# A decoder layer's index scores for the sample: TensorE in written order, with projections in pieces of three matmuls between transposes, products and head sums

## The chip, the core and the metric

The kernel runs on one core of a Trainium2 chip. The core has five engines with a queue each: PE (TensorE, matrix products and transposes), DVE (VectorE), ACT (ScalarE), POOL (GpSimd) and SP (which only issues transfers here). The metric is the device time of one execution in microseconds (us), the median of several runs.

## The reference, cut to what matters

One step of a hybrid decoder layer: 1024 tokens of a prompt and 8 samples of 4 new tokens with 8192 old keys each. The stage in question computes, for the sample's tokens, the index scores by which the 256 best keys are chosen; the same is done for the prompt.

```python
def _index_select(qi, wi, ki, qpos, kpos, topk):
    s = jnp.einsum('bqhd,bsd->bqhs', qi, ki) * (D_IDX ** -0.5)
    score = jnp.einsum('bqh,bqhs->bqs', wi, jax.nn.relu(s))
    valid = kpos[None, None, :] <= qpos[None, :, None]
    score = jnp.where(valid, score, -jnp.inf)
    top_val, top_idx = lax.top_k(score, topk)
    return top_idx, jnp.isfinite(top_val)

def _dsa_sample(qa, ka, va, qi, ki, wi, cache_k, cache_v, cache_kidx, page_table, rel_bias):
    ki_past = cache_kidx[page_table].reshape(B, past, D_IDX)
    ki_all = jnp.concatenate([ki_past, ki], axis=1)
    idx, ok = _index_select(qi, wi, ki_all, qpos, kpos, topk)
    ...
```

Ahead of it stand the RMSNorm and one input projection (`z = h @ w_in`, split into `qa, ka, va, qi, ki, wi, ga, qb, kb, vb, gb`); behind it the attention over the chosen keys, the retention heads, gates, output projection and a gated embedding.

## The kernel before, in words

A scheduler (Tile) puts the written instructions into an order for each engine, by priorities and its own estimates; where the program says `issue_after`, it pins one behind another. Every engine then works through its list without looking ahead: an instruction that waits holds up all behind it.

The stage is the loop over 8 samples `b` and two halves `a` (L797 to L838), 16 half-iterations. A half-iteration gathers 128 pages of index keys with a GpSimd transfer (`kx`, L801), turns them on PE in two blocks of 8 transposes (`ptx`, L810; a PSUM pair, two of them), copies each block to SBUF on ACT (`kT`, L811; two buffers), and multiplies with the queries in 8 matmuls (`pox`, L817). These fill two PSUM banks, the even matmuls one and the odd ones the other; ACT applies relu to each bank (`rl`, L826). After two half-iterations the heads are summed: `head_sum`, 4 matmuls into `py` (L772, L775), an ACT copy `ys`, a store to `xt_d`; and later `by_key`: 4 transposes `pxt` (L784), 8 small copies `xe` on DVE (L789), a store to `xs_d`. The two are kept in a list `pend` and one is taken out per half-iteration (`later`).

PSUM has two banks of the kind "t" at this time. `pox` takes both, and `pxt`, and the transposes `kvt` of the key and value projections (L404, inside `use_kv`), take one each. So a `pxt` bank has to be emptied by DVE's `xe` before the `pox` that comes next can write into it.

Beside this two other chains run. The unit generator (`units`) projects `qa`, `ka` and `va`, and `ga`, each a `triple` of three groups of tokens (384, 384 and 288 wide), each group 24 matmuls `pb` (`proj_b`, L252 to L254: high times high, high times low, low times high). `unit(1.4)` takes 1.4 groups out of it per half-iteration. The generator `bp` (`bisect_prompt`) finds the prompt's thresholds bit by bit: 15 bits, each with 4 counts on DVE (L663), two sign counts `js` on ACT (L659), a fix-up (L667), and the next candidate (L682, L684); then a tail, nearly all on DVE: low words and maxima (L696, L698, L704), a branch (L713), and for each of six blocks of 384 to 1024 keys the final mask (L731 to L738, with the scan L735 and L736 behind it). `step(bp)` takes one step, two per half-iteration.

After the loop the sample's own search begins (`bisect_sample`), which loads `xt_d`, and the retention projections follow on PE (`pqk`, L271 and L262 to L264).

Of the kernel before, what the change touches and what calls it, by code (L numbers as in the profile page):

```python
# [22 lines left out]
NS = 32  # L23
# [97 lines left out]
def tile_step(ctx: ExitStack, tc: tile.TileContext, I, O):  # L121
# [5 lines left out]
    psum = {}  # L127

# [63 lines left out]
    def make_toep(tz):  # L192
# [8 lines left out]
        nc.tensor.matmul(pt[:, :384], rb16.rearrange("p r h -> p (r h)"), onehot, start=True, stop=True)  # L201
# [41 lines left out]
    def proj_b(w, c0, m, consume, groups=(0, 1, 2)):  # L243

        hi, lo = w[:2]
        for g in groups:
# [3 lines left out]
            for k in range(KC):  # L250
                wh, wl = hi[:, k, c0:c0 + m], lo[:, k, c0:c0 + m]
                nc.tensor.matmul(pt[:m, :n], wh, xh[:, k, ts], start=(k == 0), stop=False)  # L252
                nc.tensor.matmul(pt[:m, :n], wh, xl[:, k, ts], start=False, stop=False)
                nc.tensor.matmul(pt[:m, :n], wl, xh[:, k, ts], start=False, stop=(k == KC - 1))  # L254
            consume(g, pt)

    def mm_a(pt, lhs, w, n, tb, kc=KC):

        hi, lo = w[:2]
        for k in range(kc):  # L260
            ah, al = lhs(k, tb)
            nc.tensor.matmul(pt[:, :n], ah, hi[:, k, :n], start=(k == 0), stop=False)  # L262
            nc.tensor.matmul(pt[:, :n], ah, lo[:, k, :n], start=False, stop=False)  # L263
            nc.tensor.matmul(pt[:, :n], al, hi[:, k, :n], start=False, stop=(k == kc - 1))  # L264

    def mm_s(pt, a, w, n, sp, name, kc=KC):

        ng = min(4, kc)
        for k in range(kc):
            j = k % ng  # L270
            nc.tensor.matmul(pt[NS * j:NS * j + NS, :n], a[:, k, :], w[2][k], start=(k < ng), stop=(k >= kc - ng))  # L271
# [75 lines left out]
    def mm_qk(pt, st, kh, kl, n):  # L347
        for c in range(0, n, 512):
            w = min(512, n - c)
            nc.tensor.matmul(pt[:, c:c + w], st, kh[:, c:c + w], start=True, stop=False)  # L350
            nc.tensor.matmul(pt[:, c:c + w], st, kl[:, c:c + w], start=False, stop=True)
# [44 lines left out]
    def use_kv(g, pt, outs, outp, new):  # L396
# [3 lines left out]
        nc.scalar.copy(st[:, 0, :n], pt[:, :n])  # L400
        tp = bank("kvt", "t")
        for i in range(0, n, 128):
            rows = min(128, n - i)
            nc.tensor.transpose(tp[:rows, i:i + 128], st[:, 0, i:i + rows], ident)  # L404
# [7 lines left out]
        return tk  # L412
# [12 lines left out]
    def use_va(g, pt):  # L425
        tk = use_kv(g, pt, O["v_sample"], O["v_prompt"], vnew)
        nc.sync.dma_start(v_d[:, 3 * g:min(8, 3 * g + 3), :], tk)
# [34 lines left out]
    with pool("ix", side="right") as ix:  # L462
# [4 lines left out]
        def use_ki(g, pt):  # L467
# [6 lines left out]
            for i in range(0, n, 128):  # L474
                tb, rows = g * 3 + i // 128, min(128, n - i)
                tp = bank("kt", "t")
                nc.tensor.transpose(tp[:rows, :72], kiT[:, i:i + rows], ident[:72, :72])
# [281 lines left out]
    for h in range(8):  # L759
        nc.tensor.matmul(pn[:NS, h * 32:h * 32 + 32], qsn[:, h, :], kis, start=True, stop=True)  # L760
# [8 lines left out]
    def head_sum(b, rls):  # L769
        py = bank("py")  # L770

        last_ = nc.tensor.matmul(py[96:128, :], wst[:, b, :], rls[3], start=True, stop=True)  # L772
# [8 lines left out]
    def by_key(b, ys):  # L781
        pt = bank("pxt", "t")
        for i in range(4):
            nc.tensor.transpose(pt[:, i * 128:(i + 1) * 128], ys[:, i * 128:(i + 1) * 128], ident)  # L784
# [8 lines left out]
    def later():  # L793
        if pend:
            pend.pop(0)()

    for b in range(8):  # L797
        rls = []
        for a in range(2):
# [4 lines left out]
            kTs = []  # L804
            for up in range(2):
                pt = pair("ptx")
                kT = sx.tile([128, 1024], F32, tag="kT", bufs=2, name="kT")
                for i in range(8):
                    r2 = up * 8 + i
                    nc.tensor.transpose(pt[:, i * 128:i * 128 + 128], kx[:, r2 * 128:(r2 + 1) * 128], ident)  # L810
                nc.scalar.copy(kT, pt)  # L811
                kTs.append(kT)
            po = [bank("pox", "t") for _ in range(2)]

            def part(e, r):
                rr = slice(64 * r, 64 * r + 64)
                return nc.tensor.matmul(po[r][32 * e:32 * e + 32, :], qbd[rr, b, :],  # L817
                                        kTs[e // 2][rr, e % 2 * 512:e % 2 * 512 + 512], start=True, stop=True)

            first = part(3, 1)  # L820
            with tc.issue_after(first.ins):
                for e, r in ((3, 0), (2, 1), (2, 0), (1, 1), (1, 0), (0, 1), (0, 0)):
                    part(e, r)
            for r in range(2):
                rl = sx.tile([128, 512], F32, tag="rl", bufs=6, name="rl")
                nc.scalar.activation(rl, po[r], AF.Relu)  # L826
                rls.append(rl)
            later()
# [4 lines left out]
            unit(1.4)  # L833
        pend.append(lambda b=b, rls=rls: head_sum(b, rls))
    while pend:
        later()
    for _ in unit_gen:
        step(bp)  # L838
# [5 lines left out]
    def bisect_sample():  # L844
# [26 lines left out]
        def count(thr, op):  # L871
# [3 lines left out]
            nc.tensor.matmul(t, group, cnt, start=True, stop=True)  # L875
# [7 lines left out]
        def totals():  # L883

            t = bank("stot", "t")[:, 0:4]
            nc.tensor.matmul(t, groupr, sgn, start=True, stop=True)
# [77 lines left out]
        nc.tensor.matmul(t[:, :32], group, apart.rearrange("p a b -> p (a b)"), start=True, stop=True)  # L964
# [38 lines left out]
        nc.tensor.matmul(tot, group, cnt, start=True, stop=True)  # L1003
# [3 lines left out]
        for src, dst in ((tf, tq), (need, nq)):  # L1007
            t = bank("tbc", "t")
            nc.tensor.transpose(t[:, :NS], src.to_broadcast([NS, 128]), ident[:NS, :NS])
# [54 lines left out]
    def chunk_mm(qk, vv, tb, rows, mask_ap, hp):  # L1064

        r = bank("ret", "c")
        nc.tensor.transpose(r[:, 0:rows], qk[:rows, 0:128], ident[:rows, :rows])
        nc.tensor.transpose(r[:, 128:128 + rows], qk[:rows, 128:256], ident[:rows, :rows])
# [6 lines left out]
        for j, sc in enumerate((r[:rows, 256:256 + rows], e[:rows, :rows])):  # L1075
            js = slice(j * 64, j * 64 + 64)
            nc.tensor.matmul(sc, qkT[js, 128:128 + rows], qkT[js, 0:rows], start=True, stop=True)
# [40 lines left out]
    def ret_sample(hp, qk, sh, acc):  # L1118
# [7 lines left out]
        for b in range(8):  # L1126
            o = r[NS * (b % 4):NS * (b % 4) + NS, 0:128]
            nc.tensor.matmul(o, qm[:, b, :], s0[:, b, :], start=(b < 4), stop=(b >= 4 and b % 4 > 1))
        for j in range(2):
            nc.tensor.matmul(r[NS * j:NS * j + NS, j * 64:j * 64 + 64], sm[:NS, j, :NS], vv[:NS, j * 64:j * 64 + 64],  # L1130
# [5 lines left out]
        for j in range(2):  # L1136
# [4 lines left out]
            nc.tensor.matmul(d[js], qk[:NS, 128 + j * 64:192 + j * 64], vm, start=True, stop=True)  # L1141
# [28 lines left out]
    def sample_select():  # L1170
# [41 lines left out]
        def prefix(src):  # L1212
# [8 lines left out]
            nc.tensor.matmul(t[:, :NS], low, tot, start=True, stop=True)  # L1221
# [23 lines left out]
        for c in range(0, NS * 66, 512):  # L1245
            w = min(512, NS * 66 - c)
            t = bank("pdf", "t")
            nc.tensor.matmul(t[:, :w], dif16, flat[0][:, c:c + w], start=True, stop=True)
# [3 lines left out]
        for q3 in range(0, NS, 3):  # L1252
            nqs = min(3, NS - q3)
            t = bank("psl", "t")
            for i in range(nqs):
# [3 lines left out]
                for a in range(2):  # L1259
                    nc.tensor.matmul(t[:, (2 * i + a) * 66:(2 * i + a + 1) * 66],  # L1260
# [16 lines left out]
        for g in range(2):  # L1277
# [4 lines left out]
            nc.tensor.matmul(t[:, :1], t8.rearrange("p q h -> p (q h)"), C("far"), start=True, stop=True)  # L1282
# [18 lines left out]
    def sample_attn():  # L1301
# [16 lines left out]
        def attend(p):  # L1318
# [21 lines left out]
            for j in range(2):  # L1340
                nc.tensor.transpose(t[:, j * 128:j * 128 + 128], kw[:, j, :128], ident)
# [474 lines left out]
```

## Time and profile before

| what | us |
|---|---|
| median of 3 runs | 1086.92 (1085.57 to 1087.62) |
| the profiled execution, its own time | 1089.05 |
| its span | 1087.3 |
| PE busy in it | 996.1 (92%) |
| DVE busy | 705.1 (65%) |
| ACT busy | 501.5 (46%) |

The profiled execution is one run, so its rows are to be set against its own span; it took 2.1 us more than the median. Its mean granted TensorE clock is 0.95. In rows of the timeline the first number is the start in us from the span's beginning, the second the duration; at the end, in brackets, the idle time before and what ended it. The stage lies between about 182 and 353 us.

### The profile page before, as it was taken

How to read it: one execution, taken by the hardware profiler on the slowest of the kernel's cores; microseconds unless marked ns; L12 is line 12 of the kernel's file. 1: busy time of each engine (PE TensorE's matmuls, PEld its weight loads, DVE VectorE, ACT ScalarE, POOL GpSimd, SP SyncE). 2: the span in 40 equal slices, each digit the busy share in tenths (PEclk: the TensorE clock that was granted, in tenths of full speed). 3: DMA queues.
4: the chain of work that ended last, by engine and by line, in shares of the span. 5: the costliest groups of instructions: out<-in, count | busy, mean ns of one | idle time of the engine just before them, and what ended most of it. 6: DMA issues, size and time to landing. Idle time of an engine off the chain costs nothing.

```text
span 1087.3 us, 19979 instructions
## 1 busy us (share of the span) xinstructions
PE 996.1 (92%) x7499; PEld 846.3 (78%) x7499; DVE 705.1 (65%) x2062; ACT 501.5 (46%) x1090; POOL 288.8 (27%) x285
## 2 busy tenths in 40 slices
PE   3899997888988899988999996899999899999998
PEld 2899997656865898888897884566665799999998
DVE  6847778888890566967969847677763422684332
ACT  5545564866434377532342336556554332452210
POOL 3102223102211432434613512525332321122110
PEclk8899999888988999989999995999999899999999
DMA  8211235435442411112301624524212511332211
GB/s 283 66 59 49 78 107 184 146 128 178 157 143 98 100 40 40 50 32 85 80 4 46 166 95 117 143 73 122 59 44 61 143 59 40 116 119 84 83 42 40
DMA packets 98310, 102.26 MB, mean 94 GB/s; under 512 B 21346, under 2 KB 88386, under 8 KB 95906
## 3 DMA queue, kind: packets, MB, share of 16 engines
q1 hardware_dynamic: 92450, 74.74, 23.0%
q0 software_dynamic: 5760, 26.22, 7.8%
q8 instruction: 59, 0.97, 0.4%
q14 instruction: 41, 0.34, 0.1%
HBM read 79.25 MB, written 21.68 MB: 93 GB/s over the span
## 4 chain that ended last, share of the span: by engine, by line
PE 46%; DVE 11%; issue 5%; DMA 4%; POOL 3%; ACT 3%; SPq 1%; DVEq 0%; POOLq 0%; ACTq 0%
PE pg L262 3%; PE pg L264 3%; PE pg L263 3%; PE pvg L262 3%; PE po L264 3%; PE po L262 3%; PE po L263 3%; PE ob L1592 3%; PE pvg L263 2%; PE pvg L264 2%; PE ptp L1584 2%; DMA wraw_vgb<-in_w_in 1%; PE sa L1568 1%; PE pty L1639 1%; POOL kvs L1159 1%
## 5 line engine op out<-in xcount | busy, mean ns | idle before, releaser
L1159 POOL DMA_INDIRECT kvs<-in_cache_kv,idx x64 | 64.9, 1014 | 86.2 <-ACT pT L1589 32.6
L262 PE MATMUL po<-whi_o,yTh 128*128 128x256 f32 x256 | 74.8, 292 | 4.2 <-DVE x L1679 3.7
L262 PE MATMUL pvg<-whi_vgb,xh 128*128 128x256 f32 x256 | 76.6, 299 | 2.1 <-ACT sg L1061 1.3
L262 PE MATMUL pqk<-whi_qkb,xh 128*128 128x256 f32 x256 | 75.2, 294 | 2.6 <-DVE rp L1048 2.4
L264 PE MATMUL pvg<-whi_vgb,xl 128*128 128x256 f32 x256 | 74.9, 292 | 0.0
L263 PE MATMUL pvg<-wlo_vgb,xh 128*128 128x256 f32 x256 | 74.3, 290 | 0.0
L264 PE MATMUL po<-whi_o,yTl 128*128 128x256 f32 x256 | 74.2, 291 | 0.0
L263 PE MATMUL po<-wlo_o,yTh 128*128 128x256 f32 x256 | 73.9, 289 | 0.0
L264 PE MATMUL pqk<-whi_qkb,xl 128*128 128x256 f32 x256 | 73.8, 288 | 0.0
L263 PE MATMUL pqk<-wlo_qkb,xh 128*128 128x256 f32 x256 | 73.0, 285 | 0.0
L262 PE MATMUL pg<-whi_g,yTh 128*128 128x256 f32 x256 | 72.7, 284 | 0.0
L264 PE MATMUL pg<-whi_g,yTl 128*128 128x256 f32 x256 | 72.3, 282 | 0.0
L263 PE MATMUL pg<-wlo_g,yTh 128*128 128x256 f32 x256 | 72.3, 282 | 0.0
L496 DVE SCALAR_TENSOR_TENSOR score<-r,wi,score 128x384 f32<-128x384 f32 (+5 forms) x42 | 44.2, 1053 | 20.7 <-ACT r L492 19.6
L1577 ACT ACTIVATE L<-L,mn 128x128 f32<-128x128 f32 (+7 forms) x64 | 49.5, 776 | 14.3 <-DVE mn L1574 14.1
L262 PEld LDWEIGHTS po<-whi_o,yTh 128*128 128x128 f32 x256 | 50.4, 197 | 6.0 <-DVE x L1679 3.9
L262 PEld LDWEIGHTS pqk<-whi_qkb,xh 128*128 128x128 f32 x256 | 49.4, 193 | 6.9 <-issue 5.5
L1773 DVE TENSOR_TENSOR sgm<-pu,sgm 128x256 f32<-128x256 f32 x32 | 13.6, 424 | 62.3 <-PE pu L264 55.1
L262 PEld LDWEIGHTS pvg<-whi_vgb,xh 128*128 128x128 f32 x256 | 49.3, 192 | 5.1 <-ACT sg L1061 1.8
L264 PEld LDWEIGHTS pqk<-whi_qkb,xl 128*128 128x128 f32 x256 | 49.1, 192 | 2.7 <-issue 2.4
L1584 PEld LDWEIGHTS ptp<-cst,L 128*128 128x128 f32 x288 | 31.9, 142 | 24.3 <-issue 19.6
L263 PEld LDWEIGHTS po<-wlo_o,yTh 128*128 128x128 f32 x256 | 50.2, 196 | 0.5 <-issue 0.4
(546 smaller groups left out, 3277.5 us busy)
## 6 DMA issues: line engine op xcount, KB each, us to landing
wraw_qkb<-in_w_in SPq DMA_DIRECT2D x16, 256.0 KB, 4.3
wraw_vgb<-in_w_in SPq DMA_DIRECT2D x16, 256.0 KB, 4.2
wraw_o<-in_w_out SPq DMA_DIRECT2D x8, 512.0 KB, 5.5
qas<-qas_d SPq DMA_DIRECT2D x8, 512.0 KB, 5.0
xr<-in_x_prompt SPq DMA_DIRECT2D x8, 512.0 KB, 3.8
wraw_g<-in_w_ple_gate SPq DMA_DIRECT2D x8, 512.0 KB, 4.3
out_y_prompt<-sgm SPq DMA_DIRECT2D x32, 128.0 KB, 1.7
qas_d<-qst SPq DMA_DIRECT2D x8, 384.0 KB, 2.4
```

The source lines that it names most:

```text
L262: nc.tensor.matmul(pt[:, :n], ah, hi[:, k, :n], start=(k == 0), stop=False)
L263: nc.tensor.matmul(pt[:, :n], ah, lo[:, k, :n], start=False, stop=False)
L264: nc.tensor.matmul(pt[:, :n], al, hi[:, k, :n], start=False, stop=(k == kc - 1))
L496: nc.vector.scalar_tensor_tensor(sc, r[:, :n], wi[:, qb, h:h + 1], sc, op0=ALU.mult, op1=ALU.add)
L1159: return nc.gpsimd.indirect_dma_start(out=dst, out_offset=None, in_=kvflat, in_offset=bass.IndirectOffsetOnAxis(ap=idx, axis=0))
L1568: nc.tensor.matmul(s[:, :wc], qas[:, h, :], kah[kv][:, c:c + wc], start=True, stop=False)
L1577: behind[0] = nc.scalar.activation(L[:, :n], L[:, :n], AF.Exp, bias=least, scale=-1.0, accum_out=sm[:, i4:i4 + 1])
L1584: nc.tensor.transpose(tp[:, i4 * 128:i4 * 128 + 128], P[i4][:, kb * 128:kb * 128 + 128], ident)
L1592: nc.tensor.matmul(ob[64 * o:64 * o + 64, :256], vtok[:, kb, kv * 64:kv * 64 + 64], pT[:, o * 256:o * 256 + 256], start=(kb == 0), stop=(k ...
L1639: nc.tensor.transpose(pt[:, j * 128:(j + 1) * 128], src[a][:, j * 128:(j + 1) * 128], ident)
L1773: nc.vector.tensor_tensor(sg[:rows], usrc, sg[:rows], op=ALU.mult)
```

## The change: order and size of the pieces

1. `matmul` and `transpose` are wrappers now. While `pinned[0]` is set, which it is from before the loop to after its tail, each TensorE instruction keeps the order in which it is written. (In the order of the changed kernel all of them bear the lines of the wrappers, L131 and L135.)
2. `triple` yields after every three matmuls, that is 8 times a group; `unit(rate)` outside the stage counts eight pieces for one, so nothing changes there.
3. `use_kv` copies the projection and leaves its transposes, `turn_kv`, in a list `held`; a later piece (the one with k = 2) takes one out.
4. The loop's body is written in the order in which PE is to work, with `fill(n)` laying n pieces in between, 8.4 in a half-iteration. The tail takes the rest of the pieces and the last head sums in turn.
5. The parts of `pox` and `py` stand in plain order, where one of them had been pinned ahead of the rest.

The number of TensorE instructions is the same. The diff, cut (the many lines that only turn `nc.tensor.matmul` into `matmul` are left out):

```diff
+    def matmul(*a, **k):
+        i = nc.tensor.matmul(*a, **k)
+        return tc.keep_in_program_order(i) if pinned[0] else i
...
-        tp = bank("kvt", "t")
+        held.append(lambda: turn_kv(g, st, outs, outp, new))
+
+    def turn_kv(g, st, outs, outp, new):
...
         def triple(w, c0, use):
             for g in range(3):
-                proj_b(w, c0, 128, use, (g,))
-                yield
+                pt = bank("pb")
+                t0, n = GRP[g]
+                ts = slice(t0, t0 + n)
+                for k in range(KC):
+                    wh, wl = w[0][:, k, c0:c0 + 128], w[1][:, k, c0:c0 + 128]
+                    matmul(pt[:, :n], wh, xh[:, k, ts], start=(k == 0), stop=False)
+                    matmul(pt[:, :n], wh, xl[:, k, ts], start=False, stop=False)
+                    matmul(pt[:, :n], wl, xh[:, k, ts], start=False, stop=(k == KC - 1))
+                    if k == KC - 1:
+                        use(g, pt)
+                    elif k == 2 and held:
+                        held.pop(0)()
+                    yield
...
     def unit(rate):
-        tick[0] += rate
+        tick[0] += 8 * rate
...
-        last_ = nc.tensor.matmul(py[96:128, :], wst[:, b, :], rls[3], start=True, stop=True)
-        with tc.issue_after(last_.ins):
-            for i in range(3):
-                nc.tensor.matmul(py[32 * i:32 * i + 32, :], wst[:, b, :], rls[i], start=True, stop=True)
+        for i in range(4):
+            matmul(py[32 * i:32 * i + 32, :], wst[:, b, :], rls[i], start=True, stop=True)
...
+    pinned[0] = True
+    fill(8)
     for b in range(8):
         rls = []
         for a in range(2):
...
+            kTs = [turn(kx, 0)]
+            fill(3)
+            kTs.append(turn(kx, 1))
+            fill(2)
+            if pend:
+                pend.pop(0)()
+            fill(1.7)
+            score_keys(b, kTs, rls)
+            fill(1.7)
             tickb[0] += 2
             while tickb[0] >= 1:
                 tickb[0] -= 1
                 step(bp)
-            unit(1.4)
         pend.append(lambda b=b, rls=rls: head_sum(b, rls))
-    while pend:
-        later()
-    for _ in unit_gen:
-        step(bp)
+    for n, _ in enumerate(unit_gen):
+        if n % 4 == 3 and pend:
+            pend.pop(0)()
+    step(bp, 8)
+    while held:
+        held.pop(0)()
+    while pend:
+        pend.pop(0)()
+    pinned[0] = False
```

`turn` holds the 8 transposes and the `kT` copy, `score_keys` the 8 products and two relus that stood in the loop.

Two places show what the scheduler makes of it. The first is PE, from the fourth `pxt` to the products that follow. Before (`ptx` are the page transposes, `py` the head sum, `pb` the projections, `pox` the products):

```order
L810 MATMUL ptx<-cst,kx 128x128 x4
L784 MATMUL pxt<-cst,ys 128x128 x4
L810 MATMUL ptx<-cst,kx 128x128 x12
L772 MATMUL py<-rl,wst 32x512
L775 MATMUL py<-rl,wst 32x512 x3
L252 MATMUL pb<-xh,whi_ga_2428 128x384
L253 MATMUL pb<-xl,whi_ga_2428 128x384
L254 MATMUL pb<-xh,wlo_ga_2429 128x384
...
L817 MATMUL pox<-kT,qbd 32x512 x8
```

Twenty projections, twelve transposes and a head sum stand between `pxt` and `pox`. In the changed kernel, at its fourth `pxt`:

```order
L131 MATMUL pb<-xl,whi_ga_1742 128x384
L131 MATMUL pb<-xh,wlo_ga_1743 128x384
L135 MATMUL pxt<-cst,ys 128x128 x4
L131 MATMUL pb<-xh,whi_ga_1742 128x384
...
L131 MATMUL pox<-kT,qbd 32x512 x8
L131 MATMUL pb<-xh,whi_ga_1742 128x384
...
L135 MATMUL ptx<-cst,kx 128x128 x8
```

Six projections stand between the two there, and the transposes and the head sum have moved away from the place.

The second is DVE, in the tail of `bp`, where the copies `xe` stand among the blocks of the mask. Before, the fourth and the fifth and those behind it:

```order
L735 SCALAR_TENSOR_TENSOR rk<-eq 128x768
L733 TENSOR_SCALAR need<-cnt 128x1
L789 COPY xe<-pxt 128x32 x8
L736 SCALAR_TENSOR_TENSOR eq<-rk,need,eq 128x768
...
L736 SCALAR_TENSOR_TENSOR eq<-rk,need,eq 128x1024
L737 TENSOR_TENSOR gt<-gt,eq 128x1024
L738 TENSOR_SCALAR mask<-gt 128x1024
L789 COPY xe<-pxt 128x32 x32
```

In the changed kernel (its L761 is the L735 of before, L762 is L736, L813 is L789):

```order
L761 SCALAR_TENSOR_TENSOR rk<-eq 128x512
L759 TENSOR_SCALAR need<-cnt 128x1
L762 SCALAR_TENSOR_TENSOR eq<-rk,need,eq 128x512
L813 COPY xe<-pxt 128x32 x8
...
L761 SCALAR_TENSOR_TENSOR rk<-eq 128x1024
L813 COPY xe<-pxt 128x32 x8
L759 TENSOR_SCALAR need<-cnt 128x1
...
L764 TENSOR_SCALAR mask<-gt 128x1024
L813 COPY xe<-pxt 128x32 x24
```

The fourth `xe` has moved from the block of 768 keys to that of 512, the fifth from behind the last block to the middle of it; the last three come behind all of them in both. The third, not shown, has moved in front of the low words of 896 and 1024 keys, where it had stood behind both.

More of the change, by code (lines that the diff above doesn't have):

```diff
@@ L127, in tile_step, with transpose @@
     psum = {}
+    pinned = [False]
+    def matmul(*a, **k):
+        i = nc.tensor.matmul(*a, **k)
+        return tc.keep_in_program_order(i) if pinned[0] else i
+    def transpose(*a, **k):
+        i = nc.tensor.transpose(*a, **k)
+        return tc.keep_in_program_order(i) if pinned[0] else i
     def psum_phase(**bufs):
@@ L403, in use_kv @@
             rows = min(128, n - i)
-            nc.tensor.transpose(tp[:rows, i:i + 128], st[:, 0, i:i + rows], ident)
+            transpose(tp[:rows, i:i + 128], st[:, 0, i:i + rows], ident)
         nb = min(n, T - t0)
@@ L411, in use_kv @@
             nc.sync.dma_start(outs.rearrange("o b t n d -> (o b t) (n d)"), new)
-        return tk
+        if new is vnew:
+            nc.sync.dma_start(v_d[:, 3 * g:min(8, 3 * g + 3), :], tk)
     def use_ka(g, pt):
@@ L425, in use_va @@
     def use_va(g, pt):
[L426 to L427 removed]
+        use_kv(g, pt, O["v_sample"], O["v_prompt"], vnew)
     def use_ga(j, g, pt):
@@ L451, in units @@
                 w.append(load_w(loads[i][0], wcols((loads[i][1], 256))))
+    held = []
     unit_gen = units()
@@ L759, in tile_step @@
     for h in range(8):
-        nc.tensor.matmul(pn[:NS, h * 32:h * 32 + 32], qsn[:, h, :], kis, start=True, stop=True)
+        matmul(pn[:NS, h * 32:h * 32 + 32], qsn[:, h, :], kis, start=True, stop=True)
     rn = sx.tile([NS, 8, NS], F32, name="rn")
@@ L791, in by_key, with turn, score_keys, fill @@
         nc.sync.dma_start(xs_d[:, b * 256:b * 256 + 256], xe.rearrange("p t a e u -> p (t a e u)"))
-    def later():
-        if pend:
-            pend.pop(0)()
+    def turn(kx, up):
+        pt = pair("ptx")
+        for i in range(8):
+            r2 = up * 8 + i
+            transpose(pt[:, i * 128:i * 128 + 128], kx[:, r2 * 128:(r2 + 1) * 128], ident)
+        kT = sx.tile([128, 1024], F32, tag="kT", bufs=2, name="kT")
+        nc.scalar.copy(kT, pt)
+        return kT
+    def score_keys(b, kTs, rls):
+        po = [bank("pox", "t") for _ in range(2)]
+        for e in range(4):
+            for r in range(2):
+                rr = slice(64 * r, 64 * r + 64)
+                matmul(po[r][32 * e:32 * e + 32, :], qbd[rr, b, :],
+                       kTs[e // 2][rr, e % 2 * 512:e % 2 * 512 + 512], start=True, stop=True)
+        for r in range(2):
+            rl = sx.tile([128, 512], F32, tag="rl", bufs=6, name="rl")
+            nc.scalar.activation(rl, po[r], AF.Relu)
+            rls.append(rl)
+    share = [0.0]
+    def fill(n):
+        share[0] += n
+        while share[0] >= 1:
+            share[0] -= 1
+            next(unit_gen, None)
+    pinned[0] = True
+    fill(8)
     for b in range(8):
@@ L803, in tile_step @@
                 in_offset=bass.IndirectOffsetOnAxis(ap=kidx[:, a * 8 + b:a * 8 + b + 1], axis=0))
[L804 to L827, printed above, removed]
-            later()
+            kTs = [turn(kx, 0)]
[7 more added lines that the diff above has]
+            fill(1.7)
             tickb[0] += 2
@@ L874, in count @@
             t = bank("stot", "t")[:, 0:1]
-            nc.tensor.matmul(t, group, cnt, start=True, stop=True)
+            matmul(t, group, cnt, start=True, stop=True)
             return t
@@ L885, in totals @@
             t = bank("stot", "t")[:, 0:4]
-            nc.tensor.matmul(t, groupr, sgn, start=True, stop=True)
+            matmul(t, groupr, sgn, start=True, stop=True)
             return t
@@ L1002, in bisect_sample @@
         tot = bank("stot", "t")[:, 0:1]
-        nc.tensor.matmul(tot, group, cnt, start=True, stop=True)
+        matmul(tot, group, cnt, start=True, stop=True)
         V.tensor_copy(te, tot)
@@ L1076, in chunk_mm @@
             js = slice(j * 64, j * 64 + 64)
-            nc.tensor.matmul(sc, qkT[js, 128:128 + rows], qkT[js, 0:rows], start=True, stop=True)
+            matmul(sc, qkT[js, 128:128 + rows], qkT[js, 0:rows], start=True, stop=True)
             nc.vector.tensor_tensor(sm[:rows, j, :rows], sc, mask_ap, op=ALU.mult)
@@ L1220, in prefix @@
             t = bank("pfx", "t")
-            nc.tensor.matmul(t[:, :NS], low, tot, start=True, stop=True)
+            matmul(t[:, :NS], low, tot, start=True, stop=True)
             V.tensor_tensor(tmp, end, tot, op=ALU.subtract)
@@ L1281, in sample_select @@
             V.tensor_copy(t8, tot[:, gq][:, :, None].to_broadcast([128, 16, 8]))
-            nc.tensor.matmul(t[:, :1], t8.rearrange("p q h -> p (q h)"), C("far"), start=True, stop=True)
+            matmul(t[:, :1], t8.rearrange("p q h -> p (q h)"), C("far"), start=True, stop=True)
             cf = p2.tile([128, 1], F32, tag="cf", bufs=1, name="cf")
@@ L1467, in tile_step @@
             o = r[:, 0:128]
-            nc.tensor.matmul(o, qk[:, 128:256], vv, start=True, stop=True)
+            matmul(o, qk[:, 128:256], vv, start=True, stop=True)
             nxt = sbd[(tb + 1) % 2]
```

88 lines of the change are left out of this document (44 added, 44 removed).

## The prediction

> **What bounds the kernel now.** I read the stretches first, since the share of the whole span (PE 92%) says nothing about this stage. The columns are the length, the busy time of PE, its weight loads, DVE, ACT and POOL, the granted clock and the DMA share.
>
> ```profile
> 182.00:262.00 80.00, 64.08 (x410) 45.58 (x410) 68.61 (x211) 61.16 (x102) 11.97 (x10) 0.83 0.55 180
> 262.00:309.30 47.30, 42.43 (x314) 34.48 (x310) 42.08 (x94) 18.00 (x27) 9.34 (x6) 0.97 0.39 129
> 309.30:324.50 15.20, 15.13 (x114) 11.39 (x115) 14.92 (x27) 7.31 (x11) 2.53 (x2) 0.87 0.44 140
> 324.50:353.20 28.70, 25.26 (x202) 17.51 (x200) 1.77 (x17) 12.28 (x19) 2.81 (x10) 0.90 0.32 116
> 353.20:358.00 4.80, 4.80 (x31) 3.48 (x31) 2.28 (x16) 0.36 (x1) 0.00 (x0) 0.53 0.42 121
> ```
>
> From 182 to 262 PE is idle for 16 us, and from 262 to 353 it is nearly full while DVE has nothing left after 324.5. So two kinds of work meet here: a DVE chain (the prompt's bit search and its tail) that runs to 324.5, and PE work that goes on to 353.2. The DVE rows mark the chain: first and last row of the 15 bits, one bit that nothing disturbs, then the tail with the by-key copies `xe` in it.
>
> ```profile
> 186.38 0.17 DVE L678 TENSOR_SCALAR cand<-tbits 128x6 int32<-128x6 int32 x1
> 206.15 0.17 DVE L684 SCALAR_TENSOR_TENSOR cand<-gb,cand 128x6 int32<-128x6 int32 x1
> 210.06 0.17 DVE L684 SCALAR_TENSOR_TENSOR cand<-gb,cand 128x6 int32<-128x6 int32 x1
> 248.78 2.31 DVE L682 TENSOR_SCALAR gb<-cnt 128x6 int32<-128x6 f32 x1
> 261.71 0.17 DVE L682 TENSOR_SCALAR gb<-cnt 128x6 int32<-128x6 f32 x1
> 274.11 1.00 DVE L698 SCALAR_TENSOR_TENSOR mask<-mask,t,lw 128x768 uint16<-128x768 bf16 x1
> 292.45 2.34 DVE L738 TENSOR_SCALAR mask<-gt 128x384 bf16<-128x384 bf16 x1
> 294.72 2.62 DVE L734 TENSOR_SCALAR eq<-score,tbits 128x512 bf16<-128x512 f32 x1
> 299.21 0.75 DVE L736 SCALAR_TENSOR_TENSOR eq<-rk,need,eq 128x512 bf16<-128x512 f32 x1
> 318.82 2.29 DVE L735 TENSOR_TENSOR_SCAN rk<-eq 128x1024 f32<-128x1024 bf16 x1
> 323.65 0.87 DVE L789 COPY xe<-pxt 128x32 f32<-128x32 f32 x8
> 340.54 0.88 DVE L789 COPY xe<-pxt 128x32 f32<-128x32 f32 x8 [16.02 <-PE pxt L784]
> ```
>
> An undisturbed bit is 210.06 - 206.15 = 3.91 us, and the 15 bits took 261.71 - 186.38 = 75.3. DVE stands still in them only here (total, times, longest):
>
> ```profile
> DVE cnt L667 <- ACT js L659: 4.4, 4, 2.0
> DVE xe L789 <- PE pxt L784: 3.8, 2, 2.1
> ```
>
> After 324.5 the sign turns: the sixth `xe` waits 16.02 us for PE. The place where DVE holds PE up is this one: the second of the eight products `pox` writes the PSUM bank that the last `pxt` held, and that bank comes free only when DVE has done its `xe`, which stands in DVE's order behind bit-search work.
>
> ```profile
> 303.39 1.04 PE L817 MATMUL pox<-kT,qbd 64*32 64x512 f32 x2
> 309.37 1.95 PE L817 MATMUL pox<-kT,qbd 64*32 64x512 f32 x14 [4.94 <-DVE xe L789]
> ```
>
> Everything behind it on PE waits too, 4.94 us.
>
> **The change part by part.** The number of instructions is the same; what changes is which of them stand before and behind each such gate.
>
> First the prices on PE, start to start: 128x384 projections, 128x288 projections, one block of 8 products, two blocks of 8 transposes, the 4 `pxt`, one head sum (a matrix product of 32 rows is recorded twice, so `pox` x16 is one block of 8, and a head sum is 4 matmuls, 8 records).
>
> ```profile
> 322.66 0.34 PE L253 MATMUL pb<-xl,whi_ga 128*128 128x384 f32 x1
> ...
> 325.95 0.34 PE L254 MATMUL pb<-xh,wlo_ga 128*128 128x384 f32 x1
> ...
> 316.74 0.29 PE L252 MATMUL pb<-xh,whi_ga 128*128 128x288 f32 x1
> ...
> 317.80 0.30 PE L254 MATMUL pb<-xh,wlo_ga 128*128 128x288 f32 x1
> ```
>
> ```profile
> 284.25 1.09 PE L817 MATMUL pox<-kT,qbd 64*32 64x512 f32 x16
> 285.27 0.44 PE L254 MATMUL pb<-xh,wlo_ga 128*128 128x384 f32 x1
> ...
> 286.07 1.91 PE L810 MATMUL ptx<-cst,kx 128*128 128x128 f32 x16
> 287.74 0.38 PE L252 MATMUL pb<-xh,whi_ga 128*128 128x288 f32 x1
> ```
>
> ```profile
> 296.86 0.60 PE L784 MATMUL pxt<-cst,ys 128*128 128x128 f32 x4
> 297.30 1.47 PE L810 MATMUL ptx<-cst,kx 128*128 128x128 f32 x12
> 298.70 0.62 PE L772 MATMUL py<-rl,wst 128*32 128x512 f32 x1
> ...
> 299.70 0.45 PE L252 MATMUL pb<-xh,whi_ga 128*128 128x384 f32 x1
> ```
>
> A wide projection costs 3.29/19 = 0.173, a narrow one 1.06/8 = 0.133, a product block 1.02, a transpose block 1.67/2 = 0.84, a `pxt` 0.44, a head sum 1.0 (299.70 less 298.70). Leaving one kind for the next costs about 0.1 more (the projection at 285.27, behind a product block, took 0.44 where 0.34 is the rule).
>
> *Program order and pieces of three.* In the written order the even shares (8.4 pieces a half-iteration) put no more projections in front than the scheduler did: up to the third head sum both orders have issued 168 projections since the first of `kava`. So in the bit phase PE still idles; nothing is won there. What differs is the second half. Before, twenty projections and twelve transposes lie between `pxt` and the products that wait for its `xe`; after, six. And the projections left behind the last gate are more.
>
> *The gates on DVE.* In the new order the third `xe` stands behind L698's row of 768 keys (275.1), the fourth behind L736 of 512 (299.96), the fifth behind the scan of 1024 (318.82 + 2.29 = 321.1). These hold the product blocks 8, 10 and 12. From one such block to the next PE has 15.4 us of work by the prices above (51 projections of both widths 8.2, 4 transpose blocks 3.4, a product block, a head sum and a `pxt` 2.4, 16 changes 1.5). With 0.9 for `xe` and 1.0 for the rest of the block the third gate opens at 273.5 and PE is back at block 10 by 290, where the gate opens at 298.4 (both already 2.5 earlier, below): 8 us of standing; at block 12 it is back by 315, so 4 to 5 there. The bit phase itself moves a little: the order of ACT's work in a bit changes. The rows are (busy, mean ns):
>
> ```profile
> L659 ACT ACTIVATE js<-mask,cand 128x1024 bf16<-128x1024 bf16 x15 | 17.3, 1153 | 8.0 <-DVE cand L684 5.6 <-DVE cand L678 2.3
> L659 ACT ACTIVATE js<-mask,cand 128x896 bf16<-128x896 bf16 x15 | 15.7, 1049 | 0.1
> L811 ACT COPY kT<-ptx 128x1024 f32<-128x1024 f32 x14 | 14.1, 1010 | 5.6 <-PE pox L817 5.6
> L826 ACT ACTIVATE rl<-pox 128x512 f32<-128x512 f32 x12 | 6.4, 592 | 0.0
> L659 ACT ACTIVATION_READ_ACCUMULATOR js<-mask,cand 128x1 f32 x30 | 5.8, 194 | 0.0
> ```
>
> The two sign counts of a bit take 1.15 + 1.05 + 2 x 0.19 = 2.59. With two `kT` more it is 4.6, with one `kT` and two `rl` 4.8, over the 3.91 that DVE needs; with one copy, 3.6, under it. Going through ACT's new order, eight bits are limited by ACT (39.5 in all, 4.9 each), six by DVE (26.8, their `kvt` and `xe` copies included), the first takes 4.5, and the one slow `gb` adds 2.1: 72.9, so 2.5 us less than 75.3. Bounds: all 8.2 of idle gone, or 4 us more if ACT's longer pairs fall in one bit. I take -2.5, the nearer to the rows. The fifth `xe` is then done at 321.1 - 2.5 + 0.9 = 319.5.
>
> *Work behind the fifth gate*, from the order: 84 wide projections 14.5, 48 narrow 6.4, 8 transpose blocks 6.7, four whole product blocks and seven eighths of the twelfth 5.0, 3 head sums 3.0, 3 `pxt` 1.3, some 25 changes of kind 2.5, and the last three `xe`, each between its `pxt` and the next products, 1.2. That is 40.6, so the stage ends at 360.1. Before, it ended here:
>
> ```profile
> 353.26 1.94 PE L271 MATMUL pqk<-wraw_qkb,xs 128*32 128x256 f32 x16
> ```
>
> That is +6.8. One gain comes back: before, PE enters the next stage at clock 0.53 (353.20 to 358.00, 4.80 us) because it had stood for `kT`, `rl` and `ys`; after, it arrives from a stream of projections, and the same work at near full clock takes some 2.5 to 2.8, so -2.0. Sum +4.8. I carry it to the end one for one, since what follows is PE's own work (the end of the chain of waits is PE).
>
> The Trainium skill (TensorE: Matmul & The Clock Gate, Part 1) says that TensorE falls to half clock after an idle window of about 3.4 us and needs to be warmed again. The products after the 4.94 us wait above agree: 14 records in 1.95 where 16 take 1.09. By that rule each of the stalls would cost 1 to 2 us more, of which only the one at block 12 would reach the end; my sum has none, and the upper bound holds it.
>
> *POOL and the slow DVE rows.* Three DVE rows of a third of a microsecond took 2.3 to 2.6. The two in the tail fall under this:
>
> ```profile
> 292.28 4.76 POOL L177 TENSOR_TENSOR wlo_qkb<-wraw_qkb,whi_qkb 128x1024 fp32r<-128x1024 f32 x2 [3.09 <-ACT whi_qkb L176]
> ```
>
> In the new order ACT's cast for it stands behind the eleventh products, thus behind the fourth gate. The fourth gate then opens 4 us earlier, and the fifth does not move, as the 4 us still lie before it. If they did not return at all, the fifth would open at 315.4.
>
> *The rest has one answer.* The held `kvt` transposes and their two copies, stores and the `v_d` store come a few pieces later and in the bit phase, where nobody waits for them; SP's queue gets them in another order, with hundreds of microseconds to the reader. Cover gone, they would cost DVE the same copies. The head sums' stores to `xt_d` and the `kx` gathers on POOL sit behind PE's transposes as before. The last head sum comes 18 rows before the end, and the sample's search waits for its store; PE has the retention projections meanwhile. The removed order of the product's eight parts costs nothing: they run one behind the other.
>
> **The rivals.**
>
> *A: DVE gates, as above.* For it: the 4.94 us wait exists already and the copies stand where they stand. 1086.9 + 4.8 = 1091.7; with both ends of the unknowns (-8.2 to +4 in the bits, +2 for the clock) +2 to +12.
>
> *B, the other side: the projections keep PE full.* If the gates do not bind, PE runs from 262 on without a stop. By the stretches it is idle for 4.9, 0.1 and 3.4 us up to 353.2, in all 8.4; at a full clock the rows of 0.87 and 0.90 lose 15.2 x 0.1 + 28.7 x 0.07 = 3.5 (0.97 taken as full), and the next stage's start gives 2.0: 13.9 less, 1073. It decides if the third, fourth and fifth `xe` come before PE is at blocks 8, 10 and 12. Against it: their rows on DVE. If only the fourth binds, the end falls 5 us before A's; if only the third, the end falls some 5 us before the old. The Trainium skill (Perfetto Trace Analysis, Optimization Strategy) has that where the busiest engine changes over time, interleaving the regimes may help; that is what this change does, and this rival is what it would give. The trace agrees that the regimes differ (DVE 68.61 of 80, later 1.77 of 28.7).
>
> *C: the bit search shrinks to DVE's own time.* With 6 to 8 us less in the bits, or with 4 from POOL's slow rows, the fifth gate opens at 313 to 315.5, and +4.8 becomes about 0: 1087. For it: DVE's 8.2 us idle is all there is to lose. Against: ACT's pairs.
>
> *D: the half clock at the gates slows transposes and so `kT`, `xe` and the bits.* Then the search is 4 to 8 us longer: 1099 or more. The row 0.83 in 182 to 262 speaks for some of it.
>
> That the change does nothing is out: the order shows other rows in the whole stage.
>
> **How the numbers follow.** A 0.55, B 0.08 and its partial forms 0.10, C 0.21, D 0.06. The profiled run took 1089.05 against a median of 1086.92; the sum is a difference of spans and is put on the median. Forecast 1091.7. The range leaves out full B and the far end of D: low 1081 (only the third gate binds: 1086.9 - 5 less a little of the clock), high 1099 (D's beginning, A's end). A difference of 0.2%, 2.2 us, is about what a measurement of this kernel tells from none. Of A, 0.5 lies above that and 0.05 within; C gives 0.13 within, 0.04 slower and 0.04 faster; B and its parts 0.16 faster and 0.02 within; D slower. Faster 0.20, same 0.20, slower 0.60.
>
> **What would show it.** Right: DVE busy from 186 to 318 nearly without a gap; waits of `pox` for `xe` of 4 to 9 us that end near 273, 294 to 299 and 320; the stage's first `pqk` at about 358 to 361; the clock there over 0.8. Wrong: no wait of `pox` for `xe` over 3 us, or the first `pqk` before 351. If the first `pqk` is late but the end is not, the carry to the end was wrong.

## The result and the profile after

The changed kernel took 1094.66 us (median of 15 runs, 1092.33 to 1099.98) where the kernel before took 1086.92 (15 runs, 1082.83 to 1094.12): a ratio of 1.0072, with an interval of 1.0052 to 1.0092, so some 7.8 us slower. The profiled execution took 1092.33, the lowest of its runs, with a span of 1090.6.

The stretches of the changed kernel, cut at the same times as before (length, busy time of PE, weight loads, DVE, ACT, POOL, granted clock):

```profile
182.00:262.00 80.00, 67.44 (x460) 51.13 (x459) 76.02 (x225) 63.58 (x106) 11.27 (x9) 0.92 0.54 176
262.00:309.30 47.30, 41.32 (x281) 31.30 (x280) 40.73 (x91) 18.51 (x26) 6.80 (x6) 0.89 0.41 125
309.30:324.50 15.20, 9.68 (x58) 6.58 (x56) 8.51 (x13) 3.61 (x5) 4.08 (x3) 0.78 0.23 90
324.50:353.20 28.70, 28.70 (x226) 21.78 (x219) 1.74 (x16) 12.86 (x19) 1.13 (x4) 1.00 0.36 121
353.20:358.00 4.80, 4.80 (x38) 3.78 (x36) 0.15 (x2) 1.08 (x2) 0.00 (x0) 1.00 0.26 96
```

DVE is fuller in the first stretch (76.0 instead of 68.6) and done earlier. PE has lost time in the second and third: it is idle for 6.0 and 5.5 us there (4.9 and 0.1 before) at a clock of 0.89 and 0.78. In the fourth it has no gap and the full clock, but it also still has work in the fifth, which before belonged to the next stage. The waits of PE in 182 to 362 (total, times, longest) name the place:

```profile
PE pox L131 <- DVE xe L813: 6.8, 3, 3.2
PE pox L131 <- DVE need L759: 5.5, 1, 5.5
```

The last one is named after `need`, the row that follows `xe`; the timelines of PE and DVE show that it is the fifth by-key copy, done at 315.35, with the scan of 1024 keys in front of it:

```profile
308.93 1.04 PE L131 MATMUL pox<-kT,qbd 64*32 64x512 f32 x2
315.49 1.96 PE L131 MATMUL pox<-kT,qbd 64*32 64x512 f32 x14 [5.52 <-DVE need L759]
```

```profile
308.70 5.88 DVE L761 TENSOR_TENSOR_SCAN rk<-eq 128x1024 f32<-128x1024 bf16 x1
314.51 0.84 DVE L813 COPY xe<-pxt 128x32 f32<-128x32 f32 x8
```

The stage's end and the next stage's start on PE:

```profile
180.64 1.94 PE L135 MATMUL ptx<-cst,kx 128*128 128x128 f32 x8 [4.79 <-DMA kx<-in_cache_kidx,kidx]
...
358.14 1.07 PE L131 MATMUL pqk<-wraw_qkb,xs 128*32 128x256 f32 x16
...
359.15 0.39 PE L131 MATMUL pqk<-whi_qkb,xh 128*128 128x256 f32 x1
```

The execution reached the stage 1.4 us earlier than in the profile before, where the first `ptx` stood at 182.07 and the first `pqk` at 353.26. Measured from the first `ptx` (PE's wait of 4.79 for the first gather lies ahead of it), the first `pqk` comes after 177.5 us instead of 171.2: the stage is 6.3 us longer.

### The profile page after: what moved, and what is told of

Same layout as the page of the kernel before. It is cut to its first block, busy times and chain, and to the rows that moved or that the text cites. A ratio compares the mean times of both kernels' runs of the same rounds, so it can differ in the third digit from the quotient of the medians.

```text
span 1090.6 us, 20003 instructions
## 1 busy us (share of the span) xinstructions
PE 997.8 (91%) x7499; PEld 847.7 (78%) x7499; DVE 713.3 (65%) x2062; ACT 508.1 (47%) x1094; POOL 288.1 (26%) x285
## 4 chain that ended last, share of the span: by engine, by line
PE 48%; DVE 13%; issue 5%; DMA 3%; POOL 2%; ACT 2%; SPq 1%; POOLq 0%; DVEq 0%; ACTq 0%
PE pg L131 9%; PE po L131 7%; PE pvg L131 6%; PE pqk L131 4%; PE ret L131 3%; PE sa L131 3%; PE ob L131 2%; PE ptp L135 2%; PE pu L131 2%; PE pb L131 2%; DVE rk L761 1%; DVE cx L1256 1%; DMA wraw_qkb<-in_w_in 1%; PE ls L131 1%; PE ptx L135 1%
## 5 line engine op out<-in xcount | busy, mean ns | idle before, releaser
L131 PE MATMUL pqk<-whi_qkb,xh 128*128 128x256 f32 x256 | 75.5, 295 | 5.6 <-DVE rp L1089 5.5
L131 PE MATMUL pvg<-whi_vgb,xh 128*128 128x256 f32 x256 | 76.1, 297 | 0.0
L131 PE MATMUL pvg<-whi_vgb,xl 128*128 128x256 f32 x256 | 75.8, 296 | 0.0
L131 PE MATMUL po<-whi_o,yTh 128*128 128x256 f32 x256 | 73.7, 288 | 1.8 <-DVE x L1720 1.4
L131 PE MATMUL pvg<-wlo_vgb,xh 128*128 128x256 f32 x256 | 74.9, 292 | 0.0
L131 PE MATMUL pqk<-whi_qkb,xl 128*128 128x256 f32 x256 | 74.8, 292 | 0.0
L131 PE MATMUL pqk<-wlo_qkb,xh 128*128 128x256 f32 x256 | 74.1, 290 | 0.0
L131 PE MATMUL po<-whi_o,yTl 128*128 128x256 f32 x256 | 73.3, 287 | 0.0
L131 PE MATMUL pg<-whi_g,yTh 128*128 128x256 f32 x256 | 72.8, 284 | 0.0
L131 PE MATMUL po<-wlo_o,yTh 128*128 128x256 f32 x256 | 72.6, 284 | 0.0
L131 PE MATMUL pg<-whi_g,yTl 128*128 128x256 f32 x256 | 72.4, 283 | 0.0
L131 PE MATMUL pg<-wlo_g,yTh 128*128 128x256 f32 x256 | 72.3, 283 | 0.0
L131 PEld LDWEIGHTS pqk<-whi_qkb,xh 128*128 128x128 f32 x256 | 50.0, 195 | 10.5 <-issue 8.7
L131 PEld LDWEIGHTS po<-whi_o,yTh 128*128 128x128 f32 x256 | 49.3, 193 | 3.8 <-DVE x L1720 1.6
L135 PEld LDWEIGHTS ptp<-cst,L 128*128 128x128 f32 x288 | 31.7, 142 | 25.7 <-issue 19.8
L131 PEld LDWEIGHTS pvg<-whi_vgb,xh 128*128 128x128 f32 x256 | 49.8, 194 | 1.8 <-PE pvg L131 0.8
L135 PE MATMUL ptp<-cst,L 128*128 128x128 f32 x288 | 48.3, 289 | 2.9 <-ACT L L1618 2.7
L131 PEld LDWEIGHTS pqk<-whi_qkb,xl 128*128 128x128 f32 x256 | 49.7, 194 | 1.2 <-issue 0.8
```

The source lines that it names most:

```text
L131: i = nc.tensor.matmul(*a, **k)
L135: i = nc.tensor.transpose(*a, **k)
```

## The experiments

Two theories. Theory 1 is the prediction's: `pox` waits for a PSUM bank which DVE empties late, since `xe` is queued behind bit-search rows. Theory 2: the fixed order itself costs (PE standing for transposes, `kT` and relus one after the other, and later stages planned anew). Ratios are to the kernel before on the same chip; they are the recorded ones, which differ by up to 0.3% from the quotient of the two medians. The changed kernel's is 1.0072.

**The copies on ACT.** PE's order stays as it is, row for row.

```diff
-                nc.vector.tensor_copy(xe[:, t, a].rearrange("p e (i r) -> p e i r", r=2),
+                nc.scalar.copy(xe[:, t, a].rearrange("p e (i r) -> p e i r", r=2),
```

> The changed kernel with one line altered: the 8 by-key copies xe are made by ACT, not DVE; PE's order is the same row for row. Theory 1 (the wait of pox for a bank that DVE empties behind bit-search rows): the waits of 2.2, 3.2 and 5.5 us at blocks 8, 10 and 12 go, with some 3 us of slow clock, and PE becomes the bound; ACT has three copies more in the bit phase, which gives up to 3 us back. First pqk at 343 to 347 instead of 358.1, the whole 11 to 15 us under the changed kernel, some 1081, under the kernel before as well. Theory 2 (the fixed order itself, PE standing for transposes, kT and relus in sequence, and the later stages planned anew): first pqk within 4 us of 358, the whole 1091 to 1096.

Measured: 1078.3 against 1092.2, ratio 0.9864 (0.9829 to 0.9898). The stretches and the end:

```profile
262.00:309.30 47.30, 46.75 (x372) 36.31 (x371) 42.68 (x71) 27.02 (x60) 12.43 (x8) 1.00 0.56 181
309.30:324.50 15.20, 15.20 (x124) 11.52 (x123) 3.30 (x5) 8.11 (x19) 1.95 (x3) 1.00 0.37 123
```

```profile
336.61 1.07 PE L131 MATMUL pqk<-wraw_qkb,xs 128*32 128x256 f32 x16
```

PE is full at the full clock where it stood. The first `pqk` is 21.5 us sooner than in the changed kernel, more than the 11 to 15 expected. Counted from the first `ptx`, the stage fell by 23.8 us, from 177.5 (the first row, the changed kernel) to 153.7:

```profile
180.64:358.14 177.50, 153.43 (x1055) 115.93 (x1055) 128.62 (x349) 99.63 (x158) 23.60 (x22) 0.91 0.44 146
182.94:336.61 153.67, 143.19 (x1056) 111.38 (x1056) 120.09 (x290) 105.56 (x218) 26.84 (x25) 0.95 0.52 168
```

PE's idle time fell by 13.6 us, 11 of it at blocks 8, 10 and 12. Its busy time for the same instructions fell by 10.2, at a mean clock of 0.95 instead of 0.91; the expectation had put some 3 us for the clock. In the bit phase the gate is still there, with ACT in DVE's place: at block 6 PE waits 3.3 us, where it waited 1.5 in the changed kernel.

```profile
PE pox L131 <- ACT xe L813: 3.8, 2, 3.3
```

Theory 2 is out for the stage.

**Wait or load.** The same kernel, but DVE gets 8 other copies for each sample.

```diff
+        xd = sx.tile([128, 8, 64], F32, tag="xd", bufs=1, name="xd")
+        for t in range(8):
+            nc.vector.tensor_copy(xd[:, t], ys[:, t * 64:t * 64 + 64])
```

> The changed kernel with the copies xe on ACT, and DVE given 8 other copies of 128x64 per sample instead, from ys, whose result nobody uses. It tells the wait apart from DVE's load. Theory 1: DVE may be as late as it likes, PE does not wait for it; first pqk within 3 us of the run with the copies on ACT (336.6). If it was DVE's time for the copies that mattered, the gain of 21 us goes back by the 7 us of those copies or more: first pqk at 343 or later.

Measured: ratio 0.9898 (0.9861 to 0.9934).

```profile
336.99 1.07 PE L131 MATMUL pqk<-wraw_qkb,xs 128*32 128x256 f32 x16
```

Counted from the first `ptx` the stage took 156.3 us (153.7 without the load), within the 3 us expected, with 127 us of DVE work in it instead of 120. So it is the wait, not DVE's time.

**The by-key step behind the products.** More PE work between `pxt` and the waiting `pox`.

```diff
-            if pend:
-                pend.pop(0)()
             fill(1.7)
             score_keys(b, kTs, rls)
+            if pend:
+                pend.pop(0)()
             fill(1.7)
```

> The changed kernel with head_sum and by_key taken out of the list behind the products of their half-iteration instead of ahead of them, so that a whole half-iteration (8.4 pieces, two transpose blocks) lies between pxt and the pox that waits for its bank. Theory 1: the gates stay but each comes one block of products later: the fourth xe stands behind the scan of 768 keys, the fifth behind the end of the tail (about 318), and 32.3 us of work at the prices lie behind its gate instead of 40.0; first pqk at 351 to 354, the whole 4 to 7 us under the changed kernel (1088 to 1091). Theory 2: no change beyond 2 us.

Measured: 1.003 (1.0008 to 1.0053), 4.6 us under the changed kernel; the first `pqk` came 2 us before the range expected.

```profile
349.00 1.07 PE L131 MATMUL pqk<-wraw_qkb,xs 128*32 128x256 f32 x16
```

```profile
PE pxt L135 <- ACT rl L837: 8.6, 7, 2.6
PE pox L131 <- DVE need L759: 5.1, 1, 5.1
PE pox L131 <- DVE xe L813: 0.6, 2, 0.3
```

The gates remain, but fewer of them bind (0.6 us and one of 5.1), and less lies behind the last one: 33.0 us (the products go on at 316.01) instead of 42.8. The new waits of `pxt` for relus (it stands directly behind `pox`, whose banks it needs) take something back, mostly while DVE is the bound anyway.

**More pieces early.** All projections used up by the thirteenth half-iteration: the four `fill` of a half-iteration become 4, 3, 2.2 and 2.2.

> The changed kernel with larger shares, 11.4 pieces in a half-iteration (4, 3, 2.2, 2.2) instead of 8.4, so that the projections are used up at the thirteenth and none is left for the tail. If the amount of projection work left behind the fifth gate were what counts by itself, first pqk would come some 15 us sooner, at 343. Theory 1 by the rows of the order: the gates move to earlier copies, the fourth xe now stands behind the scan of 1024 keys (315) and 40.5 us of work lie behind its block, and at the end pxt, xe, py, rl and ys follow each other with nothing between; first pqk at 356 to 361, the whole within 3 us of the changed kernel.

Measured: 1.0079 (1.0048 to 1.011), the changed kernel's time as far as the intervals tell (the two medians, 1103.95 and 1092.2, lie 1.1% apart). Counted from the first `ptx` the stage took 177.0 us, as in the changed kernel.

```profile
358.46 1.07 PE L131 MATMUL pqk<-wraw_qkb,xs 128*32 128x256 f32 x16
```

```profile
PE pox L131 <- DVE need L759: 9.8, 1, 9.8
PE pox L131 <- DVE xe L813: 4.5, 2, 3.8
```

Moving projections to the front won nothing: the waits became 9.8 and 4.5, as PE came to its gates sooner and with more of the index work still to do. It is all the work behind the gate that counts, not that of one kind.

**Without the program order.** The pieces stay, `pinned[0] = True` is left out.

> The changed kernel without the program order: the scheduler places the same pieces of three matmuls. It puts the fifth xe behind the first count of the 384 block (about 285) and the sixth behind the scan of 896 (about 305), with 24.8 us of PE work behind the latter's gate. Theory 1: DVE no longer decides the end, PE does; first pqk at 336 to 345, the whole 13 to 20 us under the changed kernel. Theory 2: the pieces, not the order, are what costs, and it stays within 3 us of the changed kernel.

Measured: 0.988 (0.9853 to 0.9907). The scheduler put each `pxt` and `xe` so that a single wait for DVE remained in the stage's second half, with PE nearly full at once:

```profile
182.00:262.00 80.00, 77.73 (x528) 54.89 (x526) 67.49 (x213) 66.45 (x111) 13.30 (x12) 0.98 0.61 200
```

```profile
345.20 1.07 PE L131 MATMUL pqk<-wraw_qkb,xs 128*32 128x256 f32 x16
```

```profile
PE pox L131 <- DVE need L759: 2.0, 1, 2.0
```

So the pieces of three by themselves don't cost; the fixed order with DVE's gates in it does. But PE is full from 182 on and yet at the first `pqk` 8.6 us behind the kernel with the copies on ACT (10.0 counted from the first `ptx`). In the whole time the two are not told apart: their intervals overlap.

**Before, and without the order, with the copies on ACT.** The same one-line edit in both.

> The kernel before with the 8 by-key copies made by ACT instead of DVE, nothing else. Theory 1 (the bank that DVE empties late): here the wait costs 4.94 us at one block and some 2 to 3 us of slow clock behind it, and the standing of the last 30 us comes from kT, rl and ys; first pqk 5 to 9 us sooner, at 344 to 348, the whole 5 to 9 us under the kernel before. If the new order were worth nothing by itself, this kernel would be as fast as the changed one with the copies on ACT (ratio 0.986); if the new order is what makes room once the gate is gone, it stays 6 us or more above that one.

Measured: 0.9968 (0.9946 to 0.999), 3.5 us less, under the 5 to 9 expected, and 6.2 us less at the first `pqk`, within them.

```profile
347.03 1.07 PE L271 MATMUL pqk<-wraw_qkb,xs 128*32 128x256 f32 x16
```

> The pieces of three without the program order, and the copies on ACT. Theory 1: without the order the gates cost only 2 us, so the move of the copies brings at most 2 to 5 us beyond the run without the order (ratio 0.988), 0.983 to 0.988. If the program order is worth something once the gates are gone, this one is not under the changed kernel with the copies on ACT (0.986).

Measured: 0.9975 (0.9955 to 0.9994), which missed the expectation: 10 us above the run with the copies on DVE, 4.9 of them at the first `pqk`; the rest came in later stages, and why stays open. PE stood for only 2.8 us of the stage and its mean clock was 0.99, but its time was longer:

```profile
299.14 1.05 PE L131 MATMUL pox<-kT,qbd 64*32 64x512 f32 x4
300.12 1.09 PE L135 MATMUL ptx<-cst,kx 128*128 128x128 f32 x8
...
302.53 1.05 PE L131 MATMUL pox<-kT,qbd 64*32 64x512 f32 x4
303.51 0.33 PE L135 MATMUL ptx<-cst,kx 128*128 128x128 f32 x1
303.77 1.06 PE L131 MATMUL pox<-kT,qbd 64*32 64x512 f32 x8
304.76 0.98 PE L135 MATMUL ptx<-cst,kx 128*128 128x128 f32 x7
...
350.13 1.07 PE L131 MATMUL pqk<-wraw_qkb,xs 128*32 128x256 f32 x16
```

A block of 8 products is 16 records and took 1.02 us as one. Here the block came in three parts: 4 records held PE for 300.12 - 299.14 = 0.98, 4 for 303.51 - 302.53 = 0.98, and 8 for 0.99. Each part cost about as much as a whole block. The groups of PE in 180 to 353, in the kernel with order and copies on ACT, then without order (busy, mean ns):

```profile
L131 PE MATMUL pox<-kT,qbd 64*32 64x512 f32 x256 | 21.9, 610 | 3.8 <-ACT xe L813 3.8
L131 PE MATMUL py<-rl,wst 128*32 128x512 f32 x64 | 8.5, 605 | 0.6 <-ACT sga L446 0.6
```

```profile
L131 PE MATMUL pox<-kT,qbd 64*32 64x512 f32 x256 | 43.6, 601 | 0.0
L131 PE MATMUL py<-rl,wst 128*32 128x512 f32 x64 | 17.9, 605 | 0.0
```

By their rows the products were busy 21.7 us longer and the head sums 9.4; in all PE was busy for 166.1 us from the first `ptx` to the first `pqk`, instead of 143.2. The kernel before with the copies on ACT has another lack: PE busy for 145.8, but of 165.0 us, with 13 us of waits for `kT`. So against these two the order that the change fixes is worth some 11 us (0.9864 against 0.9975 and 0.9968) once hardly a gate stands in it, and in the stage alone 15.2 and 11.4 us (153.7 against 168.9 and 165.0). Against the run without the order and with the copies on DVE it is 10.0 us in the stage; in the whole time that gain is not shown.

**Both edits.** The by-key step behind the products, and its copies on ACT.

> The changed kernel with both edits: the by-key step behind the products, and its copies on ACT. With the copies on ACT alone pox still waited 3.8 us for them in the bit phase and once for kvt's copy 4.5. Theory 1: the 3.8 go, the rest stays, so 0 to 4 us less than with the copies on ACT alone (first pqk 333 to 337, ratio 0.982 to 0.987); if it is slower, pxt and the relus of ACT stand in each other's way behind the products (7 such waits, 8.6 us, in the run with the step behind the products).

Measured: 0.9901 (0.9876 to 0.9927), which missed the 0.982 to 0.987 expected.

```profile
340.26 1.07 PE L131 MATMUL pqk<-wraw_qkb,xs 128*32 128x256 f32 x16
```

Not under the copies alone (336.6): the 8.6 us of `pxt` behind relus came with it again and cost more than the 3.8 that went. The lowest ratio is that of the changed kernel with the copies on ACT; the 0.988 without the order and the 0.9898 with DVE loaded have intervals that overlap with its own.

**Second profiles of both kernels**, one run each (1083.69 and 1097.63).

> The kernel before, unchanged, for a second profile. The stage should agree with the first within 1 us (first pqk 353.3 less the first page transposes 182.1: 171.2). If the passage from the last tbc to the first pdf takes 58.6 us again, the 65 to 69 us of the other kernels are the plan's; if it takes 64 or more, they are the scatter of single runs.

> The changed kernel, unchanged, for a second profile. First pqk less the first page transposes 177.5 again within 1.5 us, the fifth wait of pox for xe again 5 us or a gate within 2 us of 315 less 180.6 = 134.9 after the first page transposes; from the last tbc to the first pdf 69.0 if the plan decides that, nearer to 60 if single runs scatter.

Measured: the stage took 170.1 and 177.8 us from its first `ptx` to the first `pqk` (171.2 and 177.5 in the first profiles). The passage from the last `tbc` to the first `pdf`, in the retention stage: first the kernel before, again, then the changed kernel, again.

```profile
491.24 0.24 PE L1009 MATMUL tbc<-cst,ssm 32*128 32x32 f32 x1
550.99 0.38 PE L1248 MATMUL pdf<-eq,dif 128*128 128x512 bf16 x1
```

```profile
499.09 0.24 PE L135 MATMUL tbc<-cst,ssm 32*128 32x32 f32 x1
569.07 0.39 PE L131 MATMUL pdf<-eq,dif 128*128 128x512 bf16 x1
```

59.8 and 70.0 us, in the first profiles 58.6 and 69.0: the plan decides it, not the run. In the other eight kernels it took 64 to 69.

## Why the prediction was right, point by point

**The gate**: right. The copies on ACT took it away behind the bit phase and the stage fell by 23.8 us; other DVE work in their place brought 2.6 us back; a later by-key step and a moved share of projections acted as the rows of the orders said.

**The third and fourth gates**: the place was right, the size was not. I had PE stand 4 us or more at block 8, until 273, and 8 us at block 10, until 298 (294 if POOL's slow rows came later). It stood 2.2 and 3.2, since both gates opened sooner, at 268.5 and 290.6:

```profile
268.64 1.39 PE L131 MATMUL pox<-kT,qbd 64*32 64x512 f32 x14 [2.22 <-DVE xe L813]
...
290.78 1.96 PE L131 MATMUL pox<-kT,qbd 64*32 64x512 f32 x14 [3.21 <-DVE xe L813]
```

**The bit phase**: this term was mis-sized. I took 72.9 us for the 15 bits; from the first `cand` to the last `gb` they took 254.29 - 184.73 = 69.6:

```profile
184.73 0.17 DVE L704 TENSOR_SCALAR cand<-tbits 128x6 int32<-128x6 int32 x1
...
254.29 0.17 DVE L708 TENSOR_SCALAR gb<-cnt 128x6 int32<-128x6 f32 x1
...
283.13 0.17 DVE L748 CAST gb<-v 128x6 int32<-128x6 f32 x1 [5.63 <-DVEq L739]
```

DVE waited only 0.6 us for ACT's counts in them:

```profile
DVE cnt L693 <- ACT js L685: 0.6, 2, 0.3
```

The pairs of ACT copies that I had counted as eight slow bits lay beside DVE's own rows. The miss is even larger: two DVE rows beside POOL's cast for `ga` took 2.36 and 2.28 instead of 0.17 each, 4.3 us where I had put 2.1, so the rest of the bits took 5.5 us less than my sum. This comes close to rival C's condition (6 to 8 us less in the bits; it was 5.8), and by it alone the end would have come near the kernel before's.

**The slow DVE rows**: named, but not for this place. POOL's cast for the next weights fell under the scan in front of the fifth `xe`:

```profile
307.76 4.66 POOL L186 TENSOR_TENSOR wlo_qkb<-wraw_qkb,whi_qkb 128x1024 fp32r<-128x1024 f32 x2
```

The scan took 5.88 instead of 2.29 (5.94 in the second profile); it ended 2.2 us after the cast, about its own time. So the 3.6 us came back in one row, and the branch (the row of 283.13) took 5.63 where it had taken 4.17. The fifth gate opened at 315.35 instead of 319.5, 1.4 of it the earlier start; the stall was 5.5, forecast 4 to 5. That the cast causes the long row was only seen side by side, not tried.

**The work behind the fifth gate**: 358.14 - 315.35 = 42.8 us, forecast 40.6. The 2.2 more are the slow clock after the stall: 14 records in 1.96 and a clock of 0.78 in the stretch. From 315.49 to 320.52 the granted clock was 0.50: of these 5.0 us half, 2.5, were lost. Here the rule of the Trainium skill (TensorE: Matmul & The Clock Gate, Part 1) held as the upper bound had it: the 5.5 us stall at block 12 reached the end, and it cost about 2. But the stalls of 2.2 and 3.2 us, shorter than the window of that rule, were followed by slow rows too (14 records in 1.39 and 1.96, above; a clock of 0.54 from 269.95 to 272.92).

**The sum for the stage**: +6.8 forecast, +6.3 and +7.8 measured in the two pairs of profiles. Two errors cancelled in it: counted from the first `ptx` the fifth gate opened 2.7 us sooner than forecast, and 2.2 us more came behind it. So the mechanism was right, and that the number fits so closely is in part luck.

**The bounds of A**: wrongly summed. With -8.2 for the bits in place of -2.5 its sum is -0.9, and with +4 and 2 for the clock it is +13.3, not +2 to +12.

**The start at full clock**: right. The first `pqk` group took 359.15 - 358.14 = 1.0 us instead of 1.9, and the 4.8 us from its start on (358.14 to 362.94) have a clock of 1.00 instead of 0.53. The fifteenth row behind the group started 2.8 us after the group did instead of 4.8: the 2.0 forecast.

**The carry to the end, one for one**: right in sum in the first pair of profiles only, and in no part. From the first `pqk` to the first `pdf` the changed kernel took 206.8 and 209.6 us, the kernel before 200.5 and 200.1, so 6 to 10 us more; from there to the last `po` 398.2 and 397.2 against 406.1 and 402.4, so 5 to 8 less. Together that is -1.6 us in the first pair and +4.2 in the second, where I had put the -2.0 of the start and nothing else; the spans of the two pairs differ by 3.3 and 14.0, the medians by 7.7, and the forecast was 4.8. That the end came out near it is luck as to this part. The scheduler makes another order of the retention stage in every kernel, and that moves by as much as the forecast's size. Why the passage is shorter in the kernel before stays open.

**Rival B** was wrong in its condition, and its price came out in the sum alone: 13.9 us less if no gate binds, and with the copies on ACT it was 0.9864, 14.9 us less than the kernel before. But the stage itself gained 17.5 us (153.7 against 171.2) where B had 11.9, and the later stages gave some of it back. Interleaving, of which the Trainium skill speaks (Perfetto Trace Analysis, Optimization Strategy), does pay here, as soon as the bank between the two is emptied by an engine that isn't late.

## What to carry to other kernels

When the order on one engine is fixed by hand, look for each buffer that another engine has to empty, and read where the emptying instruction stands in that engine's queue; a program order cannot step over it as a scheduler's did. Price all work behind the last such place, not the work that was moved. If the mechanism is good but gated, move the emptying to an engine with room before giving the order up: one line turned 7.8 us lost into 14.9 won. Try the plain alternative too: without the fixed order the same pieces came to 0.988, which the whole time does not tell from it.

## What was not expected of the hardware

A product block of eight 64x32 matmuls took 1.02 us in one piece, and 0.98, 0.98 and 0.99 for its three parts when other TensorE work stood between them; a head sum's parts showed the same. In all twelve profiles the POOL cast of the next stage's weights (4.7 to 5.2 us) ran beside one or two DVE rows that then took 3.6 to 5.2 us longer than their like, whatever they were: a scan of 2.29 took 5.88, a plain mask row of 0.3 to 0.4 took 2.3 to 5.1. The cast before it, in the bit phase, cost from nothing to 4.3.
